# NaN-ignoring row maximum: a ring of 84 quarter rows, two pieces in the first 28 full tiles, and another division of the last 700 quarter rows

## The chip, the cores and the metric

The kernel runs on one core of a Trainium2 chip. The metric is the device time of one execution in microseconds (us), lower being better.

## The reference

```python
x = np.random.randn(32, 2048, 2048).astype(np.float32)   # 10% of the elements are NaN
out = np.nanmax(x, axis=-1).astype(np.float32)
```

There are 65536 rows of 2048 f32 numbers, 536.9 MB to be read once, and 65536 maxima to be written.

## The kernel before, in words

A row is cut into four quarter rows of 512 elements (Q). Each of the 128 partitions holds 512 rows, so there are 2048 quarter rows a partition; all counts below are of quarter rows a partition, and one of them is 2 KB there.

**Stages.** [...] Only the upper 16 bits of each element are touched. (1) SP issues a **load** (L307) of a stretch of quarter rows into a buffer in SBUF. (2) ACT writes, for one piece of it, a 16-bit **key** of each element into a key buffer (the call at L375, told as L226 in the profile: `kt<-xt`), an order-reversing map in which NaN falls on the other side. (3) The **back step** turns keys into upper halves again, in the place where the element lay (`xt<-kt`): on POOL (L236), or on ACT (L226 too, by `release`, L348) for pieces written with a minus sign in the lists. (4) DVE takes the maximum of whole rows (**reduce**, `tensor_reduce`, L243) into `acc`. At the end `find` (L245) puts the flag of all-NaN rows right, and six stores (L452) write the result.

**Order.** All of it is written out by hand, instruction by instruction, through the class `Order`. `add` gives an instruction the waits that its dependencies need: an engine's own semaphore counts its finished instructions (`order_pool`, `order_act`, `order_dve`), a load has one of 14 lanes, and two back steps on POOL and ACT that are needed by the same reduce share a semaphore of their own. `needed` leaves out what the engine has already seen. Each engine runs its instructions in the order in which they were added.

**Tiles.** `TILES` has, for each tile, the sizes of its loads, its pieces (key and back step each; a tuple is one key with several back steps) and its reduces. The first tile has 4 quarter rows, the others 28. The usual tile is `([28], [7, 9, 12], [16, 12])`; every eighth at first is `([28], [9, 12, -7], [8, 20])`, with a back step on ACT. Towards the end the tiles are cut finer. There are three tile buffers `xt0` to `xt2` of 28 quarter rows (`WIDE`, `BUFS`), used in turn: the loads of a tile wait for the last reduce of the tile three before (`free`). There are three key buffers of 12 (`KEYS`, `NKEYS`): a piece that doesn't fit moves on to the next one, and its key waits for the back steps that used it (`kold`). One further rule stands at L372 to L374: the key of a tile's last piece waits also for the back steps of the key buffer after its own, so that the first key of the next tile needs to wait for its load alone.

Of the kernel before, what the change touches and what calls it, by code (L numbers as in the profile page):

```python
# [8 lines left out]
D = 2048  # L9

Q = D // 4

TILES = (
    [([4], [4], [4])]
    + [([28], [7, 9, 12], [16, 12])] * 7
    + [([28], [9, 12, -7], [8, 20])]
    + [([28], [7, 9, 12], [16, 12])] * 7  # L20
    + [([28], [9, 12, -7], [8, 20])]
    + [([28], [7, 9, 12], [16, 12])] * 7
    + [([28], [9, 12, -7], [8, 20])]
    + [([28], [7, 9, 12], [16, 12])] * 7
    + [([28], [9, 12, -7], [8, 20])]
    + [([28], [7, 9, 12], [16, 12])] * 7
    + [([28], [9, 12, -7], [8, 20])]
    + [([28], [7, 9, 12], [16, 12])] * 7
    + [([28], [6, 10, 12], [16, 12])] * 3
    + [([28], [7, 9, 12], [16, 12])]  # L30
    + [([28], [6, 10, 12], [16, 12])] * 3
    + [([28], [7, 9, 12], [12, 16])] * 2
    + [([28], [7, 10, 11], [12, 16])]
    + [([28], [6, 10, 12], [16, 12])] * 3
    + [([28], [8, 11, 9], [8, 8, 12])]
    + [([20, 8], [11, -6, 6, 5], [16, 12])]
    + [([20, 8], [12, (-4, 7), 5], [8, 8, 12])]
    + [([17, 11], [12, (-4, 6), 6], [4, 12, 12])]
    + [([16, 12], [11, -5, 5, 7], [16, 12])]
    + [([13, 15], [9, -4, 7, 8], [12, 8, 8])]  # L40
    + [([14, 14], [9, -4, 4, 4, 7], [12, 8, 8])]
    + [([11, 10, 7], [5, 6, (-3, 7), 7], [4, 4, 4, 8, 8])]
    + [([11, 9, 8], [4, 7, (-2, 7), 6, -2], [4, 4, 4, 8, 8])]
    + [([8, 7, 6, 7], [3, 5, 7, (3, -3), 3, 4], [8, 4, 8, 8])]
    + [([6, 5, 6, 5, 6], [5, (5, -1), (-1, 5), 5, 3, 3], [4, 4, 4, 4, 4, 4, 4])]
    + [([5, 6, 5, 4, 4, 3, 1], [(-2, 3), 3, 3, (4, -1), 4, 4, -2.0, 2], [4, 4, 3, 1, 4, 4, 4, 4])]
    + [([4, 4, 3, 2, 4, 2, 3, 3, 3], [2, 2, 4, (-2.0, 1), 2, 3, 3, (-1, 2), (1, -1, 1), 2, -1.0], [4, 4, 4, 4, 4, 4, 4])]
)

GROUPS = [TILES[i : i + 15] for i in range(0, 60, 15)] + [TILES[60:73], TILES[73:]]  # L50


# [3 lines left out]
APART = (70, 71, 72, 73)  # L56
WIDE = 7
BUFS = 3

KEYS = 3 * D  # L60
NKEYS = 3
# [3 lines left out]
LANES = 14  # L65


# [10 lines left out]
def total(pieces):  # L78
    return sum(sum(map(abs, p)) if isinstance(p, tuple) else abs(p) for p in pieces)


def joints(pieces, reds):

    flat = []
    at = 0  # L90
    for step, parts in enumerate(pieces):
        for c in parts if isinstance(parts, tuple) else (parts,):

            flat.append((at, at + abs(c), c < 0, step + isinstance(c, float)))
            at += abs(c)
    needs = []
    done = 0
    for n in reds:
        over = [i for i, (a, b, _, _) in enumerate(flat) if a < done + n and b > done]
        done += n  # L100
        pools = [i for i in over if not flat[i][2]]
        backs = [i for i in over if flat[i][2]]
        if pools and backs and flat[pools[-1]][3] > flat[backs[-1]][3]:
            backs = []
        needs.append(pools[-1:] + backs[-1:])
    pairs = {}
    for need in needs:
        if len(need) == 2 and all(sum(i in n for n in needs) == 1 for i in need):
            for i in need:
                pairs[i] = tuple(need)  # L110
    return pairs
# [61 lines left out]
def kernel(  # L173
# [6 lines left out]

# [14 lines left out]
    rows = [sum(sum(loads) for loads, _, _ in g) * Q // D for g in GROUPS]  # L203
    assert R == P * sum(rows)
# [8 lines left out]
    xts = [sing.tile([P, WIDE * D], i32, name=f"xt{i}") for i in range(BUFS)]  # L213
    kts = [sing.tile([P, KEYS], u16, name=f"kt{i}") for i in range(NKEYS)]
    accs = sing.tile([P, sum(rows)], f32, name="acc")
    nones = flag.tile([P, sum(rows)], i32, name="none")
    late = sing.tile([P, rows[LATE]], i32, name="late")

    with tc.tile_critical():  # L219
        order = Order(nc)  # L220

        def act(deps, pair=None, **kw):
            return order.add(
                "act",
                nc.scalar,
                lambda: nc.scalar.activation(**kw),  # L226
                deps,
                lane=pair,
                joint=pair is not None,
            )  # L230

        def pool(deps, pair=None, **kw):
            return order.add(
                "pool",
                nc.gpsimd,
                lambda: nc.gpsimd.tensor_scalar(**kw),  # L236
                deps,
                lane=pair,
                joint=pair is not None,
            )  # L240

        def dve(deps, do, **kw):
            return order.add("dve", nc.vector, lambda: do(**kw), deps)  # L243
# [26 lines left out]
        act([e_warm], out=warm, in_=warm, func=ACT.Prelu, alpha=0.5)  # L270

        free = [[] for _ in range(BUFS)]
        kfree = [[] for _ in range(NKEYS)]
        clock = 0

        def last(uses):

            return list({back: e for back, _, e in sorted(uses, key=lambda u: u[1])}.values())

        key = 0  # L280
        used = KEYS
        number = 0
        lanes = [[] for _ in range(LANES)]
        turn = 0
        stores = []
        ready = []
        flagged = 0
        r0 = 0
        for gi, (s, g) in enumerate(zip(rows, GROUPS)):
            xg = xr[r0 : r0 + P * s].rearrange("(p s) d -> p (s d)", p=P)  # L290
            og = of[r0 : r0 + P * s].rearrange("(p s) -> p s", p=P)
            r0 += P * s
            first = sum(rows[:gi])
            acc = accs[:, first : first + s]
            base = 0
            for loads, pieces, reds in g:
                assert sum(loads) == total(pieces) == sum(reds)
                xt, before = xts[number % BUFS], free[number % BUFS]
                number += 1
                landed = []  # L300
                at = 0
                for c in loads:
                    c *= Q
                    e = order.add(
                        "sp",
                        nc.sync,
                        lambda: nc.sync.dma_start(  # L307
                            out=xt[:, at : at + c], in_=xg[:, base + at : base + at + c]
                        ),
                        before + lanes[turn],  # L310
                        lane=f"load{turn}",
                        step=16,
                    )
                    lanes[turn] = [e]
                    turn = (turn + 1) % LANES
                    landed.append((at, at + c, e))
                    at += c
                clean = []
                after = []
                at = done = 0  # L320
                reds = [n * Q for n in reds]
                part = []
                held = []
                pairs = {}
                if number not in APART:
                    pairs = joints(pieces, [n // Q for n in reds])
                flat = sum((p if isinstance(p, tuple) else (p,) for p in pieces), ())
                half = {}
                piece = 0

                def cleaned(a, b, k, i, e):

                    nonlocal clock
                    clock += 1
                    both = [(a, b, k, flat[i] < 0, clock)]
                    if i in pairs:
                        if pairs[i] not in half:
                            half[pairs[i]] = both
                            return
                        both += half.pop(pairs[i])  # L340
                    for a, b, k, back, when in both:
                        kfree[k].append((back, when, e))
                        clean.append((a, b, e))

                def name(i):
                    return f"pair{number}_{pairs[i][0]}" if i in pairs else None

                def release():  # L348
                    for a, b, k, kp, e, i in held:
                        e = act(  # L350
                            [e],
                            name(i),
                            out=xt[:, a:b].bitcast(i16)[:, 1::2],
                            in_=kp,
                            func=ACT.Copy,
                            bias=float(TOP),
                            scale=-1.0,
                        )
# [139 lines left out]
```

## Time and profile before

| | |
|---|---|
| median of 3 runs | 1252.75 us (1252.7 to 1253.27) |
| the profiled execution | 1252.86 us, its span 1251.1 us |
| loads | 536.87 MB, mean 429 GB/s over the span |
| DVE busy | 1110.8 us, 181 instructions |
| ACT busy | 965.5 us, 273 instructions |
| POOL busy | 1168.4 us, 242 instructions |

The span is that of the engines' instructions in one profiled execution; the time has a little more around it, 1.76 us here. A row of a group has the engine, the operation, the names and shapes of output and input, the number of instructions, the busy time in all and the mean in ns, and then the idle time just before them with what ended it. An entry of the timeline has a start, a length, the instruction and the idle time before it, and may merge several instructions. A shape of 128x512 in a key or back step is one quarter row; a reduce with 128x2048 in its input has four.

### The profile page before, as it was taken

What the parts mean: (1) busy time and instruction counts of PE and PEld (TensorE: products, weight loads), DVE (VectorE), ACT (ScalarE), POOL (GpSimd) and SP (SyncE); (2) the same over time, 40 slices, a digit from 0 to 9 for tenths busy, and PEclk for the clock granted to TensorE, in tenths of its full rate; (3) what the DMA queues carried; (4) which work ended last, traced back from release to release, by engine and by line L of the source; (5) the groups of instructions that cost most, each with busy time, mean ns of one, the idle gap of its engine ahead of it and who ended that gap; (6) DMA issues with size and microseconds to landing.
All of it is one profiled execution on the core that took longest, in us unless ns stands there. A gap on an engine that the chain in (4) does not pass through costs nothing.

```text
span 1251.1 us, 893 instructions
## 1 busy us (share of the span) xinstructions
DVE 1110.8 (89%) x181; ACT 965.5 (77%) x273; POOL 1168.4 (93%) x242
## 2 busy tenths in 40 slices
DVE  0888989888889888898988888998888899999999
ACT  3777887778777877788777877777777778999997
POOL 2999989998999899998999899999999999989998
DMA  9999999999999999999999999999999999999997
GB/s 415 438 416 436 440 440 436 415 440 440 438 433 420 440 440 436 433 422 440 440 436 433 422 440 438 438 433 422 440 438 437 435 422 436 427 438 428 429 428 298
DMA packets 15992, 537.20 MB, mean 429 GB/s; under 512 B 2545, under 2 KB 2545, under 8 KB 3569
## 3 DMA queue, kind: packets, MB, share of 16 engines
q1 hardware_dynamic: 15984, 537.14, 99.4%
q14 instruction: 8, 0.06, 0.0%
HBM read 536.87 MB, written 0.26 MB: 429 GB/s over the span
## 4 chain that ended last, share of the span: by engine, by line
DMA 40%; DVE 29%; POOL 22%; ACT 9%; issue 1%; SPq 0%
DMA xt<-in_x_dram 40%; DVE acc L243 29%; POOL xt L236 22%; ACT kt L226 8%; ACT xt L226 1%; SPq L307 0%; DVE none L249 0%; DVE acc L263 0%; SPq L493 0%; SPq L219 0%
## 5 line engine op out<-in xcount | busy, mean ns | idle before, releaser
L236 POOL TENSOR_SCALAR xt<-kt 128x3584 int16<-128x3584 uint16 (+11 forms) x236 | 1167.3, 4946 | 77.9 <-ACT kt L226 64.0
L243 DVE TENSOR_REDUCE acc<-xt 128x3 f32<-128x6144 f32 (+4 forms) x175 | 1107.6, 6379 | 136.6 <-POOL xt L236 129.1
L226 ACT ACTIVATE kt<-xt 128x3584 uint16<-128x3584 int16 (+9 forms) x247 | 913.3, 3734 | 278.3 <-DMA xt<-in_x_dram 258.3
L226 ACT ACTIVATE xt<-kt 128x512 int16<-128x512 uint16 (+6 forms) x24 | 52.9, 2202 | 0.7
L226 ACT ACT_TABLE_LOAD x1 | 1.3, 1283 | 0.9 <-SPq L219 0.9
L243 DVE TENSOR_REDUCE xt<-xt 128x1 f32<-128x1536 f32 x1 | 1.7, 1739 | 0.0
L269 DVE MEMSET scalars<- 128x1 f32 x1 | 0.1, 59 | 1.0 <-SPq L219 1.0
L249 DVE TENSOR_SCALAR none<-acc 128x414 int32<-128x414 f32 (+1 forms) x2 | 0.8, 381 | 0.1
L263 DVE TENSOR_TENSOR acc<-acc,none 128x414 int32<-128x414 int32 (+1 forms) x2 | 0.7, 374 | 0.1
L249 POOL TENSOR_SCALAR late<-acc 128x91 int32<-128x91 f32 x1 | 0.5, 547 | 0.1
L263 POOL TENSOR_TENSOR acc<-acc,late 128x91 int32<-128x91 int32 x1 | 0.3, 342 | 0.1
L479 POOL MEMSET const-float32-0.0<- 128x1 f32 x1 | 0.1, 98 | 0.2 <-issue 0.2
L226 ACT ACTIVATE scalars<-scalars 128x1 f32<-128x1 f32 x1 | 0.2, 203 | 0.0
L479 POOL MEMSET const-bfloat16-1.0<- 128x1 bf16 x1 | 0.1, 101 | 0.0
L479 POOL MEMSET const-uint8-127<- 128x1 uint8 x1 | 0.1, 101 | 0.0
L479 POOL MEMSET const-float32-1.0<- 128x1 f32 x1 | 0.1, 98 | 0.0
## 6 DMA issues: line engine op xcount, KB each, us to landing
xt<-in_x_dram SPq DMA_DIRECT2D x61, 7168.0 KB, 22.6
xt<-in_x_dram SPq DMA_DIRECT2D x2, 5120.0 KB, 17.5
xt<-in_x_dram SPq DMA_DIRECT2D x3, 2816.0 KB, 22.6
xt<-in_x_dram SPq DMA_DIRECT2D x4, 2048.0 KB, 22.3
xt<-in_x_dram SPq DMA_DIRECT2D x5, 1536.0 KB, 29.1
xt<-in_x_dram SPq DMA_DIRECT2D x2, 3584.0 KB, 24.7
xt<-in_x_dram SPq DMA_DIRECT2D x6, 1024.0 KB, 26.8
xt<-in_x_dram SPq DMA_DIRECT2D x3, 1792.0 KB, 30.0
```

What stands on the lines that cost most here:

```text
L226: lambda: nc.scalar.activation(**kw),
L236: lambda: nc.gpsimd.tensor_scalar(**kw),
L243: return order.add("dve", nc.vector, lambda: do(**kw), deps)
L249: lambda: engine.tensor_scalar(out=none, in0=acc, scalar1=NONE, scalar2=float(0x00800000), op0=ALU.is_equal, op1=ALU.mult,),
L263: lambda: engine.tensor_tensor(out=bits, in0=bits, in1=none, op=op),
L269: e_warm = order.add("dve", nc.vector, lambda: nc.vector.memset(warm, 1.0), [])
L479: nc = _bacc.Bacc("TRN2", target_bir_lowering=False, num_devices=1)
```

## The change

The three tile buffers become one ring `xt` of 84 quarter rows (`RING`), which starts at place 80 (`AT`), and the three key buffers one buffer `kt` of 36 (`KEYS`). `TILES` is replaced by three lists that run over the whole stream: `LOADS` (sizes of loads), `PARTS` (pieces, with the engine of the back step: P for POOL, A for ACT, V for DVE, which is new; a number after it says by how many further keys ACT's back step is put off; + joins a part to the key of the one before) and `REDS` (sizes of reduces). A load waits for the reduces that covered its places 84 quarter rows earlier (`given`).

In the first 28 tiles of 28 quarter rows the pieces are 12 and 16, the reduces 12 and 16, and all back steps are POOL's. Tiles 29 to 47 have the sizes of before (7, 9, 12, with 9, 12, 7 twice); the stream from tile 48 on is divided anew, with loads of 28 down to tile 57 and smaller ones after.

A key's places are the next free ones, or from 0 where they would run over the end (`room`). Its waits are those of its load, of the back steps that held its places, and, in place of the rule of L372, those of the pieces that follow within `AHEAD` quarter rows: one following piece where the key waits neither for a load nor for places, all of them where it waits for places. There are 20 lanes of loads in place of 14, and every store waits for the last load.

The diff, cut to its core:

```diff
-TILES = (
-    [([4], [4], [4])]
-    + [([28], [7, 9, 12], [16, 12])] * 7
...
-    + [([28], [6, 10, 12], [16, 12])] * 3
...
-    + [([5, 6, 5, 4, 4, 3, 1], [(-2, 3), 3, 3, (4, -1), 4, 4, -2.0, 2], [4, 4, 3, 1, 4, 4, 4, 4])]
-    + [([4, 4, 3, 2, 4, 2, 3, 3, 3], [2, 2, 4, (-2.0, 1), 2, 3, 3, (-1, 2), (1, -1, 1), 2, -1.0], [4, 4, 4, 4, 4, 4, 4])]
-)
...
-WIDE = 7
-BUFS = 3
-KEYS = 3 * D
-NKEYS = 3
+LOADS = (
+    []
+    + [4]
+    + [28] * 57
+    + [20, 23, 21, 20, 21, 26, 17, 20, 14, 15, 15, 10, 15, 15, 11, 8, 9, 9, 11, 10, 10]
+    + [8] * 6
+    + [7, 5, 5, 6, 5, 4, 4, 4, 3, 2, 4, 3, 3, 3, 2, 3, 2, 1, 2, 3, 2, 3, 2, 2]
+)
+PARTS = (
+    []
+    + ['4P']
+    + ['12P', '16P'] * 28
+    + ['7P', '9P', '12P'] * 3
+    + ['9P', '12P', '7A']
+    + ['7P', '9P', '12P'] * 7
+    + ['9P', '12P', '7A']
+    + ['7P', '9P', '12P'] * 7
+    + ['6P', '10P', '12P', '10A1', '7P', '6P', '5P', '6V', '10P', '12P', '9P', '12P', '7A', '7P', '9P', '12P']
+    + ['13P', '7P', '8A', '9P', '13P', '2A', '4A', '12P', '+6A1', '7V', '8P', '12P', '10P', '9P', '4P', '16P']
+    + ['2P', '6A', '+3A', '+9P', '4P', '11P', '8P', '2V', '3P', '+3P', '4A', '+9P', '5P', '15P', '12P', '9A']
+    + ['4P', '5P', '2P', '9P', '8P', '4A', '+9P', '7P', '9P', '6P', '8P', '+5A', '4P', '+3P', '9P', '9P']
+    + ['6A', '4P', '6P', '7P', '4P', '+4A', '4P', '5P', '6P', '8P', '3A1', '2P', '6P', '2P', '3P', '+3A']
+    + ['1P', '+3P', '6P', '4P', '2A1', '5P', '4P', '4P', '+2P', '3P', '5P', '+2A', '2P', '4P', '2A1', '4P']
+    + ['4P', '4P', '2A', '+2P', '4P', '4P', '2A1', '+2P', '4P', '3P', '1A1', '4P', '4P', '3P', '1A', '+1A1']
+    + ['+3P', '1A', '+4P', '3P', '3P', '1A1', '4P', '4P', '1A1', '3P', '4P', '3P', '2A', '2P', '1P', '1A1']
+    + ['3P', '3P', '1A', '+2P', '2P', '3P', '1A1', '+1P', '1A1', '2P', '1P', '2P', '1A1', '1P', '1P', '2P']
+    + ['2P', '2A2']
+)
+REDS = (
+    []
+    + [4]
+    + [12, 16] * 28
+    + [16, 12] * 3
+    + [8, 20]
+    + [16, 12] * 7
+    + [8, 20]
+    + [16, 12] * 9
+    + [12, 16, 3, 1, 24, 8, 4, 16, 8, 20, 8, 20, 20, 8, 12, 4, 20, 4, 16, 24, 20, 4, 20, 8, 8, 4, 16, 12]
+    + [4, 1, 3, 8, 12, 8, 8, 8, 8, 12, 8, 16, 8, 8, 8, 8, 8, 4, 4, 4, 8, 8, 8, 4, 8, 8, 4, 8]
+    + [4] * 30
+    + [2, 2, 4]
+)
+BOUNDS = (0, 396, 816, 1236, 1684, 2020)
+FLAGGED = (3, 5)
+LATE = 4
+RING = 84
+AT = 80
+KEYS = 36
+LEAD = 128
+LANES = 20
+AHEAD = 12
+TOP = 0x7F7F
+NAN = 0x7FC0
+LOW = -129
+EDGE = TOP + 0.25
+NONE = -255.0 * 2.0**120
+def plan():
+    parts = []
+    at = step = 0
+    for text in PARTS:
+        p = Part(text, at)
+        step += not p.joined
+        p.step = step
+        at = p.b
+        parts.append(p)
+    needs = []
+    done = 0
+    for n in REDS:
+        over = [p for p in parts if p.a < done + n and p.b > done]
+        done += n
+        pools = [p for p in over if p.engine == "P"]
+        backs = [p for p in over if p.engine == "A"]
+        if pools and backs and pools[-1].step > backs[-1].step + backs[-1].behind:
+            backs = []
+        needs.append(pools[-1:] + backs[-1:])
+    number = 0
+    for need in needs:
+        if len(need) == 2 and all(sum(p in n for n in needs) == 1 for p in need):
+            for p in need:
+                p.pair = number
+            number += 1
+    steps = {}
+    for p in parts:
+        steps.setdefault(p.step, []).append(p)
+    return list(steps.values())
...
-    xts = [sing.tile([P, WIDE * D], i32, name=f"xt{i}") for i in range(BUFS)]
-    kts = [sing.tile([P, KEYS], u16, name=f"kt{i}") for i in range(NKEYS)]
+    xt = sing.tile([P, RING * Q], i32, name="xt")
+    kt = sing.tile([P, KEYS * Q], u16, name="kt")
+    def ring(a, b):
+        at = (AT + a) % RING
+        assert at + b - a <= RING
+        return xt[:, at * Q : (at + b - a) * Q]
...
+        def load(upto):
+            nonlocal loaded, turn
+            while loaded < upto:
+                n = loads.pop(0)
+                a, b = loaded, loaded + n
+                g = next(i for i, (lo, hi) in enumerate(groups) if lo <= a < hi)
+                lo, hi = groups[g]
+                assert b <= hi
+                xg = xr[lo // 4 * P : hi // 4 * P].rearrange("(p s) d -> p (s d)", p=P)
+                before = [given[q - RING] for q in range(a, b) if q >= RING]
+                assert None not in before
+                e = order.add(
+                    "sp",
+                    nc.sync,
+                    lambda: nc.sync.dma_start(
+                        out=ring(a, b), in_=xg[:, (a - lo) * Q : (b - lo) * Q]
+                    ),
+                    list(dict.fromkeys(before)) + lanes[turn],
+                    lane=f"load{turn}",
+                    step=16,
+                )
+                lanes[turn] = [e]
+                turn = (turn + 1) % LANES
+                landed[a:b] = [e] * n
+                loaded = b
+        def done(p, kp, e):
+            both = [(p, kp)]
+            if p.pair is not None:
+                if p.pair not in half:
+                    half[p.pair] = both[0]
+                    return
+                both.append(half.pop(p.pair))
+            for p, kp in both:
+                clean[p.a : p.b] = [e] * (p.b - p.a)
+                for k in range(kp, kp + p.b - p.a):
+                    kfree[k] = {p.engine: e}
+                    kbusy[k] = False
+        def keys(p, kp):
+            return kt[:, kp * Q : (kp + p.b - p.a) * Q]
+        def back(who, engine, p, kp, e_key):
+            e = order.add(
+                who,
+                engine,
+                lambda: engine.tensor_scalar(
+                    out=upper(p),
+                    in0=keys(p, kp),
+                    scalar1=-1.0,
+                    scalar2=float(TOP),
+                    op0=ALU.mult,
+                    op1=ALU.add,
+                ),
+                [e_key],
+                **lane(p),
+            )
+            done(p, kp, e)
+        def release(all_=False):
+            for h in list(held):
+                p, kp, e_key, left = h
+                if left > 0 and not all_:
+                    continue
+                held.remove(h)
+                e = order.add(
+                    "act",
+                    nc.scalar,
+                    lambda: nc.scalar.activation(
+                        out=upper(p),
+                        in_=keys(p, kp),
+                        func=ACT.Copy,
+                        bias=float(TOP),
+                        scale=-1.0,
+                    ),
+                    [e_key],
+                    **lane(p),
+                )
+                done(p, kp, e)
+        def reduce():
+            nonlocal reduced, cleaned, part, open_, number, flagged
+            while reds:
+                n = reds[0]
+                lo, hi = reduced, reduced + n
+                mine = [o for o in own if o[0].a < hi]
+                if any(
+                    clean[q] is None and not any(o[0].a <= q < o[0].b for o in mine)
+                    for q in range(lo, hi)
+                ):
+                    return
+                for o in mine:
+                    own.remove(o)
+                    back("dve", nc.vector, *o)
+                reds.pop(0)
+                m = max(n // 4, 1)
+                row = lo // 4
+                at = (AT + lo) % RING * Q
+                first = at - 1 if lo % 4 else at
+                end = at + n * Q
+                to = xt[:, end - 1 : end].bitcast(f32) if hi % 4 else accs[:, row : row + m]
+                e = order.add(
+                    "dve",
+                    nc.vector,
+                    lambda: nc.vector.tensor_reduce(
+                        out=to,
+                        in_=xt[:, first:end].bitcast(f32).rearrange("p (c d) -> p c d", c=m),
+                        axis=mybir.AxisListType.X,
+                        op=ALU.max,
+                    ),
+                    list(dict.fromkeys(clean[lo:hi])) + part,
+                )
+                part = [e] if hi % 4 else []
+                open_ += range(lo, hi)
+                reduced = hi
+                if hi % 4 == 0:
+                    for q in open_:
+                        given[q] = e
+                    open_ = []
...
-                    kold = []
-                    if used + c > KEYS:
-                        key = (key + 1) % NKEYS
-                        used = 0
-                        kold, kfree[key] = last(kfree[key]), []
-                        assert all(k != key for q in half.values() for _, _, k, _, _ in q)
-                        if at + c == sum(loads) * Q:
-                            kold = kold + last(kfree[(key + 1) % NKEYS])
+        def room(at, c):
+            return 0 if at + c > KEYS else at
+        def freed(at, c):
+            want = {}
+            for k in range(at, at + c):
+                for who, (s, v) in kfree[k].items():
+                    if who == "A" and order.unseen("act", [(s, v)]):
+                        n = next(
+                            (
+                                n
+                                for n in range(1, order.count["pool"] + 1)
+                                if order.past[("pool", n)].get(s, 0) >= v
+                            ),
+                            None,
+                        )
+                        s, v = (s, v) if n is None else ("pool", n)
+                    want[s] = max(want.get(s, 0), v)
+            return list(want.items())
+        for i, ps in enumerate(steps):
+            a, b = ps[0].a, ps[-1].b
+            c = b - a
+            load(b)
+            key = room(key, c)
+            assert not any(kbusy[key : key + c])
+            deps = list(dict.fromkeys(landed[a:b])) + freed(key, c)
+            late_load = order.unseen("act", landed[a:b])
+            busy = order.unseen("act", freed(key, c))
+            if busy or not late_load:
+                nxt, j = key + c, i + 1
+                while j < len(steps) and steps[j][-1].b <= b + AHEAD:
+                    n = steps[j][-1].b - steps[j][0].a
+                    nxt = room(nxt, n)
+                    if any(kbusy[nxt : nxt + n]) or nxt < key + c and nxt + n > key:
+                        break
+                    deps += freed(nxt, n)
+                    nxt, j = nxt + n, j + 1
+                    if not busy:
+                        break
+            e_key = order.add(
+                "act",
+                nc.scalar,
+                lambda: nc.scalar.activation(
+                    out=kt[:, key * Q : (key + c) * Q],
+                    in_=ring(a, b).bitcast(i16)[:, 1::2],
+                    func=ACT.Prelu,
+                    bias=EDGE,
+                    scale=-1.0,
+                    alpha=float(TOP - LOW) / (EDGE - NAN),
+                ),
+                deps,
+            )
+            kbusy[key : key + c] = [True] * c
+            for h in held:
+                h[3] -= 1
+            release()
+            for p in ps:
+                kp = key + p.a - a
+                if p.engine == "V":
+                    own.append((p, kp, e_key))
+                elif p.engine == "A":
+                    held.append([p, kp, e_key, p.behind])
+                    release(b == total)
+                else:
+                    back("pool", nc.gpsimd, p, kp, e_key)
+            key += c
+            reduce()
...
-        for (og, bits), e in zip(stores, ready):
-            last = order.add(
-                "sp",
+        for g, (a, b) in sorted(enumerate(groups), key=lambda v: (v[0] == len(groups) - 1, v[0])):
+            og = of[a // 4 * P : b // 4 * P].rearrange("(p s) -> p s", p=P)
+            bits = accs[:, a // 4 : b // 4].bitcast(i32)
+            last = order.add(
+                "sp",
+                nc.sync,
+                lambda: nc.sync.dma_start(out=og, in_=bits),
+                [ready[g], landed[-1]],
```

## The prediction

> **What bounds the kernel now.** First the page, for the engines against the transfers: POOL is the busiest engine at 93%, but the DMA row is full in every slice except the last.
>
> ```profile
> DVE 1110.8 (89%) x181; ACT 965.5 (77%) x273; POOL 1168.4 (93%) x242
> ...
> DMA  9999999999999999999999999999999999999997
> ```
>
> Then the totals of waits (engine, line, what it waited for: us, times, longest). ACT waits for loads; it is starved, so the loads set the pace. The second line is small, but it is the one that matters here: the key step (ACT, L226) held until a back step (POOL, L236) has ended.
>
> ```profile
> ACT kt L226 <- DMA xt<-in_x_dram: 258.3, 69, 15.0
> ...
> ACT kt L226 <- POOL xt L236: 19.1, 51, 0.8
> ```
>
> Then the timeline of the first full tile, to see that wait once. The keys of 7 and 9 quarter rows (one ACT entry) end at 29.89; the key of 12 stands until 30.24, which is 26.04 + 4.19, the end of the back step of 7. That is the look-ahead of L372 to L374, on an instruction of the same tile: it costs 0.36 because only the short back step of 7 is in the way. The next tile begins at 39.70, 16.93 later.
>
> ```profile
> 22.77 7.12 ACT L226 ACTIVATE kt<-xt 128x3584 uint16<-128x3584 int16 x2 [15.00 <-DMA xt<-in_x_dram]
> 26.04 16.70 POOL L236 TENSOR_SCALAR xt<-kt 128x3584 int16<-128x3584 uint16 x3 [15.73 <-ACT kt L226]
> 30.24 5.32 ACT L226 ACTIVATE kt<-xt 128x6144 uint16<-128x6144 int16 x1 [0.36 <-POOL xt L236]
> 35.65 15.14 DVE L243 TENSOR_REDUCE acc<-xt 128x4 f32<-128x8192 f32 x2 [23.02 <-POOL xt L236]
> 39.70 7.12 ACT L226 ACTIVATE kt<-xt 128x3584 uint16<-128x3584 int16 x2 [4.14 <-DMA xt<-in_x_dram]
> ```
>
> Last, durations, from the groups with shapes kept apart (512 elements are a quarter row).
>
> ```profile
> L243 DVE TENSOR_REDUCE acc<-xt 128x4 f32<-128x8192 f32 x57 | 495.1, 8686 | 115.0 <-POOL xt L236 115.0
> L236 POOL TENSOR_SCALAR xt<-kt 128x6144 int16<-128x6144 uint16 x61 | 429.5, 7041 | 5.9 <-ACT kt L226 1.2
> ...
> L226 ACT ACTIVATE kt<-xt 128x6144 uint16<-128x6144 int16 x61 | 324.6, 5321 | 17.1 <-POOL xt L236 17.1
> ...
> L236 POOL TENSOR_SCALAR xt<-kt 128x5120 int16<-128x5120 uint16 x10 | 59.1, 5906 | 2.5 <-ACT kt L226 2.5
> ...
> L226 ACT ACTIVATE kt<-xt 128x5120 uint16<-128x5120 int16 x12 | 53.5, 4456 | 2.5 <-DMA xt<-in_x_dram 2.5
> ```
>
> No ACT or POOL row has 16 quarter rows (8192 elements). The step from 10 to 12 gives 0.43 (ACT) and 0.57 (POOL) a quarter row, so a key of 16 takes 5.32 + 4 x 0.43 = 7.04 and a back step 7.04 + 4 x 0.57 = 9.31. Taken flat at the 12's rate both would be 0.06 longer, so these two are uncertain by 0.1.
>
> **Tiles 1 to 28: two pieces.** Per tile POOL does 7.04 + 9.31 = 16.35 in place of 4.19 + 5.34 + 7.04 = 16.57, ACT 12.36 in place of 12.54, DVE the same 15.2: all below the 16.91 between loads. By sums, nothing is lost. By order, much is. The key buffer has 36 places; the 12 stand at 0 to 11, the 16 at 12 to 27, and the next 12, not fitting in 28 to 39, again at 0. The key of 16 asks for its own places (back step of 16, tile before) and, with AHEAD = 12, for those of the next piece, and these are held by the back step of 12 of its **own** tile. Written out, the number awaited on POOL's semaphore is that back step's, in tiles 1 to 27; in tile 28 a 7 follows, which stands at 28, and the wait is only on tile 27.
>
> So key 16 starts when back 12 has ended, back 16 starts when key 16 has ended, and the next tile's back 12 is queued behind back 16 on POOL. Nothing overlaps in this ring of three: 7.04 + 0.01 + 7.04 + 0.07 + 9.31 + 0.08 = 23.55 a tile (the gaps are those of the chain of waits: 0.07 ACT to POOL, 0.08 POOL to POOL). The next key of 12 (5.32) fits beside back 16, if its load has landed. It has: load i+3 waits for the last reduce of tile i, 8.7 after back 16, lands some 19 later, and is wanted 9 us after that. So the loads are no longer the bound; POOL stands idle 7 us a tile and the DMA with it.
>
> First key at 22.77 as now; back 16 of tile 1 ends at 22.77 + 5.32 + 0.07 + 7.04 + 0.01 + 7.04 + 0.07 + 9.31 = 51.63, that of tile 27 at 51.63 + 26 x 23.55 = 663.9. The load of tile 30 waits for tile 27's last reduce: 663.9 + 0.03 + 8.69, and 1.0 to its first packet (the first load: issued at 0.94, first packet 1.95), so 673.7. In the packets of before, tile 30's starts at 495.5. **The shift is 178.2.** From there the loads follow each other again: the reduces of tiles 28 to 31 end 25.3, 41.5, 58.3 and 75.1 after 663.9, each about 1 us before the DMA runs dry. Uncertain: 26 x 0.1 and a microsecond for the restart, 4 us.
>
> **Tiles 29 to 48** keep 7, 9, 12 with some 9, 12, 7 on ACT: the durations and waits of before, no change in pace.
>
> **The last 700 quarter rows.** Sums first (rows above, straight lines between sizes). ACT takes more of the back steps: POOL 349 us where it had 390, ACT 391 where it had 350, DVE 387 and three back steps of its own (15 quarter rows), the loads 427 in both (four more loads at 0.07). Again nothing exceeds the loads, so the order decides. I follow the waits from B, the landing of the load that ends at quarter row 1348 (before: ACT starts on it at 818.2; after: 996.4).
> - Tile 49 (10 on ACT, 7, 6, 5): the key of 7 waits until 24.3 for the 12 before it, and only then comes ACT's back step of 10, to 33.4; its reduces end at 49.6 (before, 28 after landing would be 45.1).
> - Tile 50: DVE's own back step of 6 is queued behind those reduces, to about 53; the key of 12 waits for it through the look-ahead, so back 12 ends at 65.4 and the reduce at 74.1. Tile 53's load waits for that and should be out by 66: the DMA loses 8.
> - Tile 55's key of 18 stands until 132.4, and one of 18 at row 1602 until 186.4, for a back step of 16 (9.3); POOL idles 7 us behind it. The loads into places 0 to 46 go out 6.5 and 3 late.
> - Row 1684 is reduced, and its flags found, at B + 260.4. Before, that is 1034.1 - 818.2 = 215.9: 44.5 later.
> - From there DVE is the bound: 64 reduces by 0.138 + 0.534 a quarter row are 204.6, and 0.4 for the flags. Before it took 1248.5 - 1034.1 = 214.4, so 9.4 is won back.
>
> **The tail costs 35.** DVE's back step isn't in the trace: by TENSOR_REDUCE a quarter row is 0.53, which I took; the bounds are zero and that of POOL (0.57), and only the 6 of tile 50 lies on this path, so 3.4 at most are in it. The Trainium skill, "VectorE: DVE Perf Modes", section "What auto-detection actually checks", has an operation with a single source and its destination in SBUF take two elements a cycle; by that the six would cost half, and the sum would be 1.7 less; no row shows it. My bounds for the tail are 22 to 43, a step followed wrongly being worth one back step (4 to 9 us).
>
> The end itself: the last load is of 2 quarter rows, one reduce of 4 follows, as before; the six stores wait for the last load, behind which five hide while DVE ends, so 2.6 from the last flag to the end stays.
>
> **Sum**, against the profiled execution (span 1251.1, time 1252.86, the median of the runs 0.11 below): 1252.86 + 178.2 + 35 = **1466**.
>
> **Rivals.**
> - *The tail keeps to the loads.* The sums of every engine allow it, and a ring that can be refilled at any place frees space sooner. Then 1252.86 + 178.2 = 1431. Against: the four places above are waits written in the program. 0.12.
> - *The hold is covered; the loads stay the bound everywhere.* This is the other side. It decides at 32.4 from landing to last reduce (two loads of 16.91, less 1.4 for issue and landing). Without the hold: 5.32 + 7.12 + 9.39 + 8.7 = 30.5, and the loads never stop. Then only the end changes: five stores (1.0 of packets) off the loads' path, four loads more (0.3): about 1252. Against: with the hold 37.7. For: only that the hold costs 0.4 now. 0.02.
> - *Larger instructions win.* POOL is the busiest engine and gets 0.22 less a tile, 28 x 0.22 = 6: 1246.7, if POOL were the bound. Against: the full DMA row. 0.01. The Trainium skill, "Perfetto Trace Analysis", section "Optimizing Scalar/DVE Operations", says that grouping into larger operations helps a saturated engine, which is this case, and also that breaking up helps where an engine causes bubbles on others, which is mine.
> - *Worse:* POOL's 8192 elements off the line, or the restart leaving gaps of a few us in each of tiles 32 to 48: 1485 or more. 0.04.
>
> **Chances and range.** My case 0.81. A measurement tells about 0.2% (2.5 us) from no change. Faster 0.01, same 0.02, slower 0.97. My own case is 1466 with -13 - 4 and +8 + 4: 1449 to 1478; down to 1430 the range takes in the first rival.
>
> **What would show it.** Right: POOL waiting for ACT's key of 16 some 7 us in each of 27 tiles (190 us in all), ACT waiting for POOL 11 us in each (23.55 less 12.36); 23.5 us between tiles and a DMA row of 7s up to about 670 us, 9s after; then gaps near 1065 and 1210; DVE without idle at the end. Wrong in the first part: a DMA row of 9s from the start. Wrong in the tail: an end at 1431, or row 1684's flags found much before 1257.

## The result, and the profile after

The changed kernel takes 1466.17 us (median of 5, 1464.98 to 1467.57) where the kernel before takes 1252.94 (median of 5): a ratio of 1.1702, 95% interval 1.1685 to 1.1719. Its profiled execution took 1466.17, with a span of 1464.4. The prediction was 1466.

First the page of the changed kernel: the busy times, and the DMA row of 40 slices.

```profile
DVE 1125.0 (77%) x196; ACT 982.1 (67%) x278; POOL 1133.4 (77%) x227
...
DMA  9868686777868686778999999999979998999995
```

POOL has fallen from 93% to 77% of the span, and no other engine has come up in its place. The DMA row, full before, stands at 6 to 8 up to slice 18 (about 660 us), then at 9, with dips in the slices that start at 1062 and 1208 us. The totals of waits of the same kernel (what waited for what: us, times, longest) say who holds whom.

```profile
ACT kt L474 <- POOL xt L343: 370.3, 57, 11.3
DVE acc L401 <- POOL xt L343: 325.5, 58, 22.5
POOL xt L343 <- ACT kt L474: 308.8, 67, 17.8
ACT kt L474 <- DMA xt<-in_x_dram: 89.0, 23, 15.0
```

Before, ACT waited 258.3 for loads and 19.1 for POOL; now it waits 89.0 for loads and 370.3 for POOL, while POOL waits 308.8 for ACT. Two engines that wait for each other so much take turns. The timeline of the first tiles shows them do it (start, length, instruction, idle before it).

```profile
22.73 5.32 ACT L474 ACTIVATE kt<-xt 128x6144 uint16<-128x6144 int16 x1 [14.97 <-DMA xt<-in_x_dram]
28.13 7.00 POOL L343 TENSOR_SCALAR xt<-kt 128x6144 int16<-128x6144 uint16 x1 [17.83 <-ACT kt L474]
35.16 12.24 ACT L474 ACTIVATE kt<-xt 128x8192 uint16<-128x8192 int16 x2 [7.12 <-POOL xt L343]
...
42.27 16.41 POOL L343 TENSOR_SCALAR xt<-kt 128x8192 int16<-128x8192 uint16 x2 [7.14 <-ACT kt L474]
...
58.72 12.24 ACT L474 ACTIVATE kt<-xt 128x8192 uint16<-128x8192 int16 x2 [11.31 <-POOL xt L343]
```

The key of 12 ends at 28.05; the key of 16 stands until 35.16, which is 28.13 + 7.00 and 0.03 more: the end of the back step of 12 of its own tile. POOL then waits 7.14 for that key. The next key of 16 starts at 58.72, 23.56 later. And the groups with shapes kept apart give the two durations that no row of before had.

```profile
L343 POOL TENSOR_SCALAR xt<-kt 128x8192 int16<-128x8192 uint16 x29 | 269.7, 9300 | 193.8 <-ACT kt L474 193.7
...
L474 ACT ACTIVATE kt<-xt 128x8192 uint16<-128x8192 int16 x29 | 203.9, 7030 | 305.3 <-POOL xt L343 305.3
```

### The profile page after: what moved, and what is told of

It is laid out like the page before. It is cut to its first block, busy times and chain, and to the rows that moved or that the text cites. A ratio compares the mean times of both kernels' runs of the same rounds, so it can differ in the third digit from the quotient of the medians.

```text
span 1464.4 us, 903 instructions
## 1 busy us (share of the span) xinstructions
DVE 1125.0 (77%) x196; ACT 982.1 (67%) x278; POOL 1133.4 (77%) x227
## 4 chain that ended last, share of the span: by engine, by line
POOL 46%; ACT 22%; DVE 20%; DMA 10%; issue 1%; SPq 0%; ACTq 0%
POOL xt L343 46%; ACT kt L474 21%; DVE acc L401 20%; DMA xt<-in_x_dram 10%; ACT xt L365 2%; DVE xt L343 0%; DVE xt L401 0%; DVE none L249 0%; DVE acc L263 0%; SPq L311 0%; ACTq L174 0%; SPq L551 0%; SPq L237 0%
## 5 line engine op out<-in xcount | busy, mean ns | idle before, releaser
L343 POOL TENSOR_SCALAR xt<-kt 128x8192 int16<-128x8192 uint16 (+11 forms) x221 | 1132.4, 5124 | 321.1 <-ACT kt L474 308.8
L401 DVE TENSOR_REDUCE acc<-xt 128x3 f32<-128x6144 f32 (+6 forms) x185 | 1106.7, 6033 | 335.2 <-POOL xt L343 325.5
L474 ACT ACTIVATE kt<-xt 128x8192 uint16<-128x8192 int16 (+12 forms) x240 | 909.0, 3834 | 467.7 <-POOL xt L343 370.3
L365 ACT ACTIVATE xt<-kt 128x512 int16<-128x512 uint16 (+9 forms) x36 | 77.1, 2148 | 0.6
L343 DVE TENSOR_SCALAR xt<-kt 128x3072 int16<-128x3072 uint16 (+2 forms) x3 | 13.7, 4550 | 0.2 <-ACT kt L474 0.2
L401 DVE TENSOR_REDUCE xt<-xt 128x1 f32<-128x1536 f32 (+2 forms) x3 | 3.6, 1208 | 0.0
```

Of the source, the lines that this page charges most:

```text
L343: lambda: engine.tensor_scalar(out=upper(p), in0=keys(p, kp), scalar1=-1.0, scalar2=float(TOP), op0=ALU.mult, op1=ALU.add,),
L365: lambda: nc.scalar.activation(out=upper(p), in_=keys(p, kp), func=ACT.Copy, bias=float(TOP), scale=-1.0,),
L401: lambda: nc.vector.tensor_reduce(out=to, in_=xt[:, first:end].bitcast(f32).rearrange("p (c d) -> p c d", c=m), axis=mybir.AxisListType.X, ...
L474: lambda: nc.scalar.activation(out=kt[:, key * Q : (key + c) * Q], in_=ring(a, b).bitcast(i16)[:, 1::2], func=ACT.Prelu, bias=EDGE, scale= ...
```

## The experiments

The stages are taken apart with one switch. The look-ahead is the added wait of a key for the places of the *following* piece; with `AHEAD = 0`, or with a condition on `b` (the end of the key's piece; tile 28 ends at 788), a key waits for its load and its own places only.

**No look-ahead up to tile 28** (`e1`):

```diff
-            if busy or not late_load:
+            if (busy or not late_load) and b > 788:
```

> The changed kernel without the look-ahead in tiles 1 to 28: a key there waits for its load and for its own places alone. Pieces, loads, reduces and the later tiles stay. Theory (the hold of the key of 16 behind the back step of 12 of its own tile is the whole cost of the first stage): tiles come every 16.91 us from the start, the shift of 178 is gone, and the time is 1466 - 178 = 1288, all that is left over 1253 being the new division of the end. Rival (two large pieces are too long a chain for a ring of three tiles, hold or not): landing to last reduce stays above 32.4, tiles come slower than 16.91, and the time stays over 1320.

Measured: 1300.22, ratio 1.0377 [1.0362, 1.0393]. Of the 178 that the first stage lost, 166 are gone with one condition, so the hold is the cause; but 1300 is 12 more than expected. In the packets of the trace the loads of tiles 1 to 30 follow each other every 17.30 us (5.02 to 506.87), where before it was 16.92. That is 11.4 by tile 30, with no hold left. The next runs take this up.

**Three pieces in the first 28 tiles** (`e3`): the usual pieces of before, 7, 9, 12, in every one of these tiles (before, every eighth is 9, 12, 7 with ACT), all the rest of the change kept. The edit in the short form of the changed kernel's lists:

```diff
-    + ['12P', '16P'] * 28
+    + ['7P', '9P', '12P'] * 28
-    + [12, 16] * 28
+    + [16, 12] * 28
```

> The changed kernel with 7, 9, 12 (reduces 16, 12) in tiles 1 to 28; ring, look-ahead and the end as changed. Theory (the look-ahead costs by the back step that it waits for: that of 7 in place of that of 12): 1288 again, with the key of 12 held 0.4 a tile. Rival (the ring itself, its waits by place or its look-ahead, is at fault, not the pieces): stays over 1400.

Measured: 1286.6, ratio 1.0271 [1.0254, 1.0288], as expected. The ring and the look-ahead cost nothing in the first 28 tiles when the key of 12 has only the short back step of its tile's first piece to wait for (0.3 to 0.4 each time): the first packet of tile 30 comes at 495.38, before at 495.47. What remains comes behind them.

**The end of before in the ring** (`e4`): two pieces up to tile 28, the sizes of before from tile 48 on (their loads, pieces and reduces in the form of the new lists).

```diff
-    + ['6P', '10P', '12P', '10A1', '7P', '6P', '5P', '6V', '10P', '12P', '9P', '12P', '7A', '7P', '9P', '12P']
...
+    + ['9P', '12P', '6P', '10P', '12P', '6P', '10P', '12P', '6P', '10P', '12P', '7P', '9P', '12P', '6P', '10P']
...
```

> The changed kernel with the loads, pieces and reduces of before from quarter row 1320 on, written in the new lists; the first 28 tiles as changed. Theory (the new division costs 35 us by itself): 1466 - 35 = 1431, a few us more if the look-ahead holds keys in the old division too. Rival (the end is slow because the slow first stage hands it a backlog): stays within 5 of 1466.

Measured: 1454.31, ratio 1.1610 [1.1592, 1.1627]: 12 less than the changed kernel, not 35. Both readings miss. The end of before, put in this ring, also loses: about 23.

**Both together** (`e6`): the condition of `e1` and the end of `e4`.

> Both: no look-ahead in tiles 1 to 28, two pieces there, and the division of before from quarter row 1320 on. Theory (hold and division are the two costs, and they add): 1253, within 6 above (the look-ahead in tile 39 and in the old division). Rival (the costs overlap, or the ring has a third cost): 1265 or more. If two pieces in themselves saved time, it would show here as less than 1251.

Measured: 1288.21, ratio 1.0283 [1.0268, 1.0299], a miss by 35. It is 166.1 below `e4`, as `e1` is 165.95 below the changed kernel, so the hold of the first stage is one separate term, and most of what is lost behind it is not in the new sizes.

**The ring alone** (`e5`): all sizes of before, with the ring, the key buffer of 36 and the look-ahead. **The same without look-ahead** (`e8`):

```diff
-AHEAD = 12
+AHEAD = 0
```

> The ring, the one key buffer and the look-ahead of the changed kernel, with all loads, pieces and reduces of before. Theory (the look-ahead, not the ring, makes the old division 20 us slower in the run with the old end and slow start): 1253 + 20 and some us more for the five tiles of 9, 12, 7: 1270 to 1285. Rival (the 20 came from the slow first stage): 1253 to 1258.

> As the ring alone with all sizes of before, but AHEAD = 0: no key waits for another piece's places. Theory: the loads are the bound again and the time is that of before, 1253 within 3. Rival (the ring's own waits cost: places reused in another order than the three key buffers): still 1265 or more.

Measured: 1292.14, ratio 1.0314 [1.0299, 1.0330], and 1253.82, ratio 1.0008 [0.9999, 1.0018]. The waits of ACT's keys for POOL, first in the ring alone, then without look-ahead:

```profile
ACT kt L476 <- POOL xt L345: 126.9, 72, 6.6
```

```profile
ACT kt L476 <- POOL xt L345: 0.7, 1, 0.7
```

With the same sizes, the look-ahead alone costs 38.3; the ring without it costs nothing that can be measured. In before the rule held only the key of a tile's last piece; in the ring it can hold any key but one that waits for its load alone.

**The changed kernel without look-ahead** (`e2`), and **three pieces without look-ahead** (`e9`, which is `e3` with `AHEAD = 0`):

> The changed kernel with AHEAD = 0 throughout; two pieces in tiles 1 to 28, the new end. From the run without look-ahead in the first 28 tiles alone (1300): if the new end's cost of some 32 us is made by the look-ahead, 1300 - 32 = 1268, the 15 left being the late loads of the two-piece stage; if it is made by the division itself (large pieces that wait for a back step still running on their own places, DVE's back steps in its queue), 1290 or more.

> 7, 9, 12 in tiles 1 to 28, AHEAD = 0, the new end. If the look-ahead makes the cost of the new end: 1253 within 5, less than 1252 if the new division then saves time. If the division itself makes it: 1275 or more.

Measured: 1268.94, ratio 1.0128 [1.0113, 1.0143], and 1253.66, ratio 1.0010 [1.0000, 1.0020]. So the new end, with its lists as they are, costs nothing beside the end of before (1253.66 and 1253.82). And two pieces, with their reduces of 12 and 16 in place of 16 and 12, cost 15.3 of their own, with no look-ahead in the program. The page of `e2` shows why this one is easy to miss: the DMA row, the rate in each slice, and the queue's share.

```profile
DMA  9999999999999999999999999999999999999997
GB/s 410 424 434 418 433 427 422 425 427 418 429 417 420 413 427 431 420 427 434 434 434 434 434 434 433 434 434 433 405 435 431 424 428 438 428 429 433 430 426 288
...
q1 hardware_dynamic: 16560, 537.14, 99.0%
```

The row is all 9s, as before, and the queue is busy 99.0% of the span (99.4% before). But the mean rate of the first 16 slices, where two pieces are used, is 423; in the ten slices from the nineteenth on it is 434. The same row of the kernel before has 433 in its first 16 slices:

```profile
GB/s 415 438 416 436 440 440 436 415 440 440 438 433 420 440 440 436 433 422 440 440 436 433 422 440 438 438 433 422 440 438 437 435 422 436 427 438 428 429 428 298
```

The queue is never idle for long, but the packets themselves take longer: over tiles 4 to 29 that makes 7.9 of the 10.5 by which the first packet of tile 30 comes later than before. The last section has more numbers.

**Sixteen first** (`e11`): the order of the two pieces turned round, look-ahead kept.

```diff
-    + ['12P', '16P'] * 28
+    + ['16P', '12P'] * 28
-    + [12, 16] * 28
+    + [16, 12] * 28
```

> The changed kernel with the pieces of tiles 1 to 28 in the other order, 16 then 12, reduces likewise. The look-ahead now falls on the key of 16, which waits with its load for the places of the next 12, held by the back step of 12 of the tile before. Theory (what counts is that key 16, back 16 and back 12 stand in one line, whichever tile holds the places): the cycle is back 12, key 16, back 16, back 12 again, 7.04 + 9.31 + 7.04 and gaps, 23.55 a tile as before the swap, and the time 1465 within 4. Rival (only a wait on the same tile's step costs, a wait on the tile before is covered): some 1300, as without the look-ahead.

Measured: 1468.39, ratio 1.1719 [1.1697, 1.1740]. The hold moves (now the key of 16 waits for the back step of 12 of the tile before) and the cycle stays at 23.55: the two lengths form one closed chain in either order.

**No look-ahead behind tile 28** (`e7`): the counterpart of `e1`.

```diff
-            if busy or not late_load:
+            if (busy or not late_load) and b <= 788:
```

> The changed kernel with the look-ahead kept in tiles 1 to 28 and left out after them. Theory (the two costs are separate, one on each side of tile 28): 1466 less the 31 between 1300 and 1269 is 1435, within 4. Rival (the backlog of the slow stage costs at the end too): over 1440.

Measured: 1434.94, ratio 1.1452 [1.1431, 1.1473]. With the others this makes a square (us):

| | look-ahead behind tile 28 | none behind tile 28 |
|---|---|---|
| look-ahead up to tile 28 | 1466.17 | 1434.94 (`e7`) |
| none up to tile 28 | 1300.22 (`e1`) | 1268.94 (`e2`) |

The rows differ by 166.0 in either column, the columns by 31.2 and 31.3 in either row. The two costs add; 15.3 is left for the two pieces (1268.94 to 1253.66), and 0.7 to the kernel before (1252.94). One hold of the second stage, in the timeline of the changed kernel at tile 39 (7, 9, 12; the tile behind it, 40, is 9, 12, 7 on ACT), and tile 39 in `e7`:

```profile
848.35 9.58 POOL L343 TENSOR_SCALAR xt<-kt 128x3584 int16<-128x3584 uint16 x2 [0.23 <-ACT kt L474]
857.96 9.26 ACT L474 ACTIVATE kt<-xt 128x6144 uint16<-128x6144 int16 x2 [5.76 <-POOL xt L343]
...
863.36 19.57 POOL L343 TENSOR_SCALAR xt<-kt 128x6144 int16<-128x6144 uint16 x3 [5.44 <-ACT kt L474]
870.42 8.62 ACT L474 ACTIVATE kt<-xt 128x6144 uint16<-128x6144 int16 x2 [3.20 <-POOL xt L343]
```

```profile
845.42 12.34 ACT L474 ACTIVATE kt<-xt 128x3584 uint16<-128x3584 int16 x3 [4.62 <-DMA xt<-in_x_dram]
```

In the changed kernel the key of 12 of tile 39 starts 5.76 after ACT was free, when the back step of 9 of its own tile is done: the 9 that follows, of tile 40, would take over places of that 9. POOL then idles 5.44 for the key. The key of 12 of tile 40 is held likewise, 3.20, for the back step of 12 of tile 39. In `e7` the three keys of tile 39 are one entry without a gap.

**Two repairs** (`e10`), to beat the kernel before: `e9` with the DVE back step of tile 50 put on POOL, because the load of tile 53 goes out late, and the last reduces turned round.

```diff
-    + ['12P', '10A1', '7P', '6P', '5P', '6V', '10P', '12P', '9P', '12P', '7A', '7P', '9P', '12P', '13P', '7P']
+    + ['12P', '10A1', '7P', '6P', '5P', '6P', '10P', '12P', '9P', '12P', '7A', '7P', '9P', '12P', '13P', '7P']
...
-    + [4, 4, 4, 4, 4, 4, 4, 4, 4, 2, 2, 4]
+    + [4, 4, 4, 4, 4, 4, 4, 4, 4, 4, 2, 2]
```

> Three pieces in tiles 1 to 28, no look-ahead, the new end with two edits: the back step of 6 of tile 50 on POOL in place of DVE, and the last reduces 4, 2, 2 in place of 2, 2, 4. From 1253.7 for the kernel without the edits: the load of tile 53 is issued 0.95 ahead there, the DMA idles 0.3 and the load is 0.7 longer, so 1.0 less; the last reduce is one of 2 (1.2) in place of 4 (2.3), so 1.1 less: 1251.6, just under the kernel before (1252.7). If DVE or ACT is late at the end for another reason, 1252.5 or more.

Measured: 1254.15, ratio 1.0011 [1.0002, 1.0020], a miss. The load of tile 53 was as late as before (first packet 0.95 after issue): POOL's extra back step of 6 took the time that DVE's had. And the last three reduces, first of `e9`, then of `e10`:

```profile
1243.75 1.21 DVE L403 TENSOR_REDUCE xt<-xt 128x1 f32<-128x1024 f32 x1
...
1245.00 3.54 DVE L403 TENSOR_REDUCE acc<-xt 128x1 f32<-128x1025 f32 x2
```

```profile
1244.54 2.29 DVE L403 TENSOR_REDUCE acc<-xt 128x1 f32<-128x2048 f32 x1 [0.47 <-POOL xt L345]
...
1246.74 1.21 DVE L403 TENSOR_REDUCE xt<-xt 128x1 f32<-128x1024 f32 x1
1247.99 1.22 DVE L403 TENSOR_REDUCE acc<-xt 128x1 f32<-128x1025 f32 x1
```

In `e9` the reduce of 2 starts at 1243.75, while POOL is still at its last work; in `e10` the reduce of 4 has to wait for it 0.47, and all ends at 1249.21 where it was 1248.54. The split row had filled time in which DVE would have stood.

**Tiles 49 and 50 in plain pieces** (`e12`): `e9` with 6, 10, 12 in both, no back step on ACT or DVE there.

```diff
-    + ['12P', '10A1', '7P', '6P', '5P', '6V', '10P', '12P', '9P', '12P', '7A', '7P', '9P', '12P', '13P', '7P']
+    + ['12P', '6P', '10P', '12P', '6P', '10P', '12P', '9P', '12P', '7A', '7P', '9P', '12P', '13P', '7P', '8A']
...
-    + [12, 16, 12, 12, 16, 3, 1, 24, 8, 4, 16, 8, 20, 8, 20, 20]
+    + [12, 16, 12, 16, 12, 3, 1, 24, 8, 4, 16, 8, 20, 8, 20, 20]
```

> The kernel of three pieces without look-ahead (1253.66 us), with tiles 49 and 50 in plain pieces of 6, 10, 12 (back steps of 16 and 12), where they have a back step of ACT and one of VectorE. Theory: the pieces of tiles 49 and 50 make the load of tile 53 late (its first packet came 0.95 us after its issue, where the others lead by over 4 us), and the restart costs 1.0 us: 1252.7 us, with tile 53's lead at 4 us or more. Rival: the load of tile 53 is late by something else, or its lateness is made good before the flags: 1253.7 us or more, with the work that leaves ACT and VectorE coming back as late GpSimd work (1254 to 1256).

Measured: 1253.16, ratio 1.0001 [0.9992, 1.0010]. The load of tile 53 leads by 3.76 again, so these pieces did make it late; the gain on `e9` is 0.5 (0.7 when each is set against its own runs of before), not 1.0. It is level with the kernel before; none of these versions beats it measurably.

## Why the prediction was right, and where it was not

**Key and back step of 16.** 7.04 and 9.31 were carried on from the step between 10 and 12; the rows have 7.03 and 9.30.

**The cycle.** 23.55 a tile was predicted; keys of 16 start at 35.16 and 58.72, and `e1` shows that the look-ahead makes it. Back step of tile 1: 51.63 predicted, 51.62 in the DVE entry that waits for it. First packet of tile 30: 673.7 predicted, 673.60 measured. This term was 178.2 and came out as 178.1. Read as a cause it has two parts: 166 for the hold, and 12 that two pieces would have cost anyway.

**Tiles 29 to 48, "no change in pace": wrong.** The step that failed is the reading that the waits of before still hold there. In the new key buffer the look-ahead to a 9, 12, 7 tile holds the key of 12 of the tile ahead of it behind that tile's own back step of 9 (the 5.76 above, at tile 39), and the loads of tiles 42 to 44 then begin late. By tile 48 its first key starts at 1001.51, 5.1 later than predicted.

**From there to the flags.** 260.4 predicted after that point, 261.4 measured, and here the path was as written out. Counted from 1001.51, the load of tile 53 goes out at 74.2 (its wait was put at 74.1), though the queue then stands empty for 6.7 and not 8; the key of 18 of tile 55 starts at 132.8 (132.4), that of row 1602 at 187.7 (186.4). Two of the named waits in full: the key of 12 of tile 50 waits 7.73 for the DVE back step (shown below), and the key of 18 at row 1602 waits 8.47 for the back step of 16, here in ACT's timeline of the changed kernel.

```profile
1189.16 7.88 ACT L474 ACTIVATE kt<-xt 128x9216 uint16<-128x9216 int16 x1 [8.47 <-POOL xt L343]
```

**The last reduces.** 205.0 predicted, 198.6 measured (1262.91 to 1461.54): 6.4 too many, mostly because the sum was of durations, and reduces in a row overlap in the profile. In the trace the 64 reduces of this stretch have durations that add up to 203.2 (204.6 by the prediction's line), but 61 of them start 0.08 before the one ahead has ended, which takes off 5.0.

So 1466 was hit with +5.1, +1.0, -6.4 and +0.3 (the end) cancelling; that the whole came out to a fraction of a microsecond is luck. The size of the tail's 35 therefore says little; its bounds of 22 to 43 hold.

**What the tail's cost was put down to: wrong.** The prediction followed single waits, several of them the look-ahead's, but treated them as brought by the new division of the last 700 quarter rows. `e4` and `e6` failed on that. `e5` and `e8` show that the old sizes in the same ring lose 38.3 over the whole kernel through the look-ahead; `e9` shows that the new division alone loses nothing measurable. Of the 35, 31.2 are the look-ahead (`e7`); the other 4 stay without it, and what makes them was not traced. The rival that the tail keeps to the loads gave 1431; `e7` is that case with the look-ahead lifted, at 1434.94.

**The rival in which the loads stay the bound** was to be decided at 32.4 from landing to last reduce, so that 30.5 without the hold would have been safe. The chain of `e2` is as worked out: its first key starts at 22.64 and the last reduce of that tile ends at 53.2, 30.6 later. The threshold was the mis-sized term: it left 1.4 for issue and landing together, and in these runs a load needs about 3 between issue and first packet alone to keep the pace. With 30.6 the load of tile 4 has 2.4, the cost is 15.3, and `e2` is slower by over 1%. In before the same stretch is 28.0 (22.77 to 50.79); of the 2.6 more, 2.1 are the last reduce, of 16 quarter rows in place of 12. Whether 16 and then 12, without look-ahead, would keep the pace was not tried.

**Larger instructions.** On the page "Perfetto Trace Analysis" of the Trainium skill, section "Optimizing Scalar/DVE Operations", the half that bears this out is that of breaking up work where an engine (Scalar or Vector there) makes others wait: two pieces in place of three cost 15.3 (`e2` against `e9`), though POOL has 0.22 less to do in each tile.

**DVE's back step: its bounds were wrong.** Zero to 3.4 was given for the 6 of tile 50; it stands at 3.61. The timeline of the changed kernel, twice:

```profile
1046.85 5.88 POOL L343 TENSOR_SCALAR xt<-kt 128x5120 int16<-128x5120 uint16 x1 [2.49 <-ACT kt L474]
1050.86 3.61 DVE L343 TENSOR_SCALAR xt<-kt 128x3072 int16<-128x3072 uint16 x1
1054.50 9.26 ACT L474 ACTIVATE kt<-xt 128x6144 uint16<-128x6144 int16 x2 [7.73 <-DVE xt L343]
```

```profile
1142.28 7.03 POOL L343 TENSOR_SCALAR xt<-kt 128x6144 int16<-128x6144 uint16 x1 [8.00 <-ACT kt L474]
...
1145.31 6.04 DVE L343 TENSOR_SCALAR xt<-kt 128x3584 int16<-128x3584 uint16 x1 [0.18 <-ACT kt L474]
```

The POOL step ends at 1052.73 and the DVE step 1.74 later; in the second fence POOL ends at 1149.31 and DVE 2.04 later. 1.74 for 6 quarter rows and 2.04 for 7 are 0.29 each; lengths of 3.61 and 6.04 would be 0.60 and 0.86. The third such step, of 2, stands at 4.00 and ends 0.60 after POOL's. So DVE is as good as blocked until POOL's instruction has ended, and then runs at 0.29, about half of a reduce's 0.53. The rule of the Trainium skill that the prediction cited ("VectorE: DVE Perf Modes", section "What auto-detection actually checks", two elements a cycle for a single source and destination in SBUF) agrees with the 0.29. The step that failed: the bounds counted the step's own work alone, and more than half of its price is the time that POOL's instruction holds it up. The Trainium skill, "SBUF — State Buffer", section "Who interferes with whom", says that such an operation, in its two-port mode, and one of GpSimd fully block each other, whoever issues first going through; the trace agrees, in 1.87 and 4.00 of blocking.

## What to carry to other kernels

A wait that is harmless for a short instruction (0.36 behind a back step of 7) can become the period of the kernel when sizes change (23.55 behind one of 12); before sizes or buffers are changed, write out for each added wait whose end it is, and whether that end lies behind the waiter in a closed chain. Sums of busy time told nothing here: no engine was over the loads' 16.91 a tile, and the tile took 23.55. And where a ring's refill was issued only 1 to 2 us before the queue ran dry, the transfers were slower in most cases although the DMA row stayed full: look at the rate beside it.

## What the runs showed of the hardware

**A load that is issued late runs below its pace.** In the packets of the trace, the 28-quarter-row load of tile 4 in three kernels (us):

| | issued | first packet | packets' time, mean of the 16 engines |
|---|---|---|---|
| before | 50.82 | 55.64, 4.8 later | 16.94 |
| `e2` | 53.24 | 55.65, 2.4 later | 17.57 |
| changed | 60.33 | 61.28, 0.95 later | 17.66 |

Taken over the loads of this size in all fourteen kernels: 448 that led by 3.0 to 5.4 take 16.93 to 17.06; 147 that led by 0.94 to 0.99, when the queue had run dry, take 17.44 to 17.96; and 195 between, by 1 to 3, scatter from 16.93 to 17.99. In `e2` tiles 4 to 30 lead by 1.0 to 2.9. A restart from an empty queue so costs the 0.95 and about 0.7 in the packets. That this goes with the lead, and not with the size of the pieces beside it, is seen in the changed kernel itself, where tiles 35 to 41 lead by 4.4 to 4.6 and take 16.93, and tiles 42 to 44, in the same stage, lead by 0.96 to 1.60 and take 17.18 to 17.88; and in tile 53, which takes 17.61 in `e9` (lead 0.95) and 16.93 in `e12` (lead 3.76). Why the packets are slower was not settled.

**The blocking goes both ways.** In `e9` POOL's back step of 12 that starts at 866.37, while DVE's back step of 6 runs from 864.38 to 868.02, is in the groups of that window with 8.56 in place of 7.03.

```profile
L345 POOL TENSOR_SCALAR xt<-kt 128x6144 int16<-128x6144 uint16 x1 | 8.6, 8557 | 0.1
```

The 1.5 that it takes longer is close to the 1.65 by which DVE's step outlasts its start. The same two steps meet so in `e2` and `e7`, where POOL's takes 8.57. The reduces, which run beside POOL all the time, keep to one duration (8686 ns for 16 quarter rows before and after). A version with DVE's back steps placed where POOL stands idle was not tried.
